# Hyena's output projection in the rings of the input projection, a finer last projection group, two pools for the convolution, and four early pairs of FFN products

## The chip, the cores and the metric

One core of a Trainium2 chip runs the whole kernel. The metric is the device time of one execution in microseconds (us). The engines are TensorE (PE: matmuls, with PEld for the weight load), VectorE (DVE), ScalarE (ACT), GpSimd (POOL) and SyncE (SP). SP and POOL issue the DMAs here, each from a queue that runs in order.

## The reference

One layer over 1024 latent tokens of width 1024, with a prefix of 256 context tokens, in float32:

```python
mod = silu(c) @ w_ada + b_ada                       # shifts, scales, gates
hc = modulate(rmsnorm(ctx), csh1, csc1)
k_c, v_c = split(hc @ w_in[:, 512:1536])
h = modulate(rmsnorm(x), sh1, sc1)
q, k, v, hv, hx1, hx2, gna, ghy = split(h @ w_in)   # w_in: 1024 x 5120
y_na = neighbourhood_attention(q, k, v, k_c, v_c, rpb)   # 8 heads of 64, windows 8 x 16 and all context keys
y_hy = hyena_mixer(hv, hx1, hx2, ...)               # order 2: z = gate[n] * long_conv_bidir(z, filter[n]), by FFT
x = x + g1 * ((sigmoid(gna) * (y_na @ w_na_o) + sigmoid(ghy) * (y_hy @ w_hy_o)) @ w_out)
h2 = modulate(rmsnorm(x), sh2, sc2)
x = x + g2 * ((silu(h2 @ w1) * (h2 @ w3)) @ w2)     # hidden 2816
return rmsnorm(x, final_g)
```

## The kernel before, in words

Each float32 operand is split into a high and a low part by one helper, `split` (L174 and L175): a cast on ScalarE, then a subtraction on VectorE. A product is then three matmuls for each 128 rows of depth (low by high, high by low, high by high), in `gemm` (L194) and in `product` (L1133).

The input projection (`project`) makes 40 blocks of 128 output channels. Each block has two halves of 512 tokens, `in_ps`, and each half is 24 matmuls of 128x512. ScalarE evacuates a half into `proj` (L601 and others), a tile of the ring "o" in the staging pool `self.stg`. The block's weights come by one 512 KB load (`wr`) in a ring of one, and are split into `wh` and `wl`. Transposed tokens (`tokens`) use the ring "tm" of the same pool.

The projection is a generator, and so are the filters, the modulation rows (`ada_rows`) and the long convolution (`conv`), which together are `side()`. The helper `_merged` advances the two in proportion: 39 projection steps to `SIDE` = 447 units of the side work. That, the scheduler's priorities and the pinned order of some matmuls set the order of instructions, in which the projection's halves lie between the small pieces of filters and convolution. When the convolution is through, `self.fine` is set, and the attention generator starts: it loads and rotates keys and queries (`kraw`, `qraw`, `kcraw` for context keys, all in a ring "raw" of two buffers), and the projection yields after the first half of a block and after the block. `AHEAD` = 5 projection steps go first, and then attention and projection take turns.

An attention step (there are 34, of which 32 have scores) issues the scores of its item (`s_ps`), the transpositions of the item before (`pt_ps`, L766), and the values of the item before that (L780). VectorE and ScalarE make the softmax between (L754, L755), and ScalarE copies `pts` (L770) and `yrow` (L787). What lies on TensorE between two such steps covers the softmax.

When the projection has ended, `hyena_out` loads the convolution's result `yhraw` in eight pieces (ring "g" of two buffers, shared with the gates `ghy`), splits it into `yhh` and `yhl`, and makes 16 products `hy_ps` of 12 matmuls. Their place is set by this rule of the attention's step number n:

```python
for n, _ in enumerate(attention):
    if n > 2 and n % 4 != 3 or n in (3, 19):
        next(hyena, None)
```

`mix` then makes `na_ps`, merges both branches by the gates and makes the output projection (`out_ps`). The FFN forms seven products of sums of the blocks of h2 and of weights in place of eight. `sums` makes those operands `h2_3` to `h2_7` on VectorE (in the profile and the order: `h_3h`, `h_3l` and so on). `ffn_early` does products that need only `h2_1` and `h2_2`, for three pairs of weight tiles w1 and w3, while the sums are made: four products of 12 matmuls (`x_ps`) a pair. Split weights lie in rings `oh` and `ol` of five. `ffn_up` follows with all the rest.

Of the kernel before, what the change touches and what calls it, by code (L numbers as in the profile page):

```python
# [10 lines left out]
F32 = mybir.dt.float32  # L11
# [12 lines left out]
SIDE = 447  # L24
# [134 lines left out]
class Block:  # L159
# [17 lines left out]
    def weights(self, pool, src, n=D, tag="w"):  # L177
        nc = self.nc
        raw = pool.tile([P, n], F32, tag=tag + "r", name=tag + "r")
        nc.sync.dma_start(raw, src)  # L180
        hi = pool.tile([P, n], F32R, tag=tag + "h", name=tag + "h")
        lo = pool.tile([P, n], F32R, tag=tag + "l", name=tag + "l")
        self.split(hi, lo, raw)
        return hi, lo
# [74 lines left out]
    def hidden(self, pool, wpool, mp, hid, w3, hT, hcT, psf):  # L259
# [42 lines left out]
        self.modulated(pool, psf, xs[0:4], 4, self.mod1[:, 0], hT[0][:, :, 0:512], hT[1][:, :, 0:512])  # L302
        normed(4, 4, "rstd1b")
        yield
        self.modulated(pool, psf, xs[4:8], 4, self.mod1[:, 0], hT[0][:, :, 512:T], hT[1][:, :, 512:T])
# [256 lines left out]
    def project(self, groups, wpool, psg, psc, hT, hcT, between):  # L562
# [8 lines left out]
        def half(f, w, st, ps, h):  # L571
# [4 lines left out]
            self.gemm(pt, w, hT, 8, 512, h * 512, self.pinned)  # L576
# [50 lines left out]
        for group in groups:  # L627
            ws = [self.ready.pop(f) for f in group]
            i = chunks.index(group[-1]) + 1
            if i < len(chunks) and chunks[i] not in self.ready:  # L630
                with self.tc.high_priority():
                    self.ready[chunks[i]] = self.weights(wpool, self.a["w_in"][chunks[i]])
# [9 lines left out]
            for f, w, st in zip(group, ws, sts):  # L642
                self.left -= 1
                finish(f, w, st)
                yield
# [3 lines left out]
    def attention(self, pool, kpool, prep, psums):  # L649
# [42 lines left out]
        def keys(pr):  # L692
            tl = tiles[pr]
            tl["kr"] = [prep.tile([P, T], F32R, tag=n, name=n, bufs=2) for n in ("krh", "krl")]
            x = prep.tile([P, 512], F32, tag="raw", name="kcraw", bufs=2)
            nc.sync.dma_start(x[:, 0:TC], self.kcd[pr])
            tl["kc"] = [prep.tile([P, TC], F32R, tag=n, name=n, bufs=2) for n in ("kch", "kcl")]
            self.split(*tl["kc"], x[:, 0:TC])
# [124 lines left out]
    def hyena_out(self, pool, wo, ps1):  # L823

        nc, a = self.nc, self.a
        yh = [pool.tile([P, 4, T], F32R, name=n, bufs=1) for n in ("yhh", "yhl")]
        for c in range(4):
            for h in range(2):
                sl = slice(h * 512, (h + 1) * 512)
                raw = pool.tile([P, 512], F32, tag="g", name="yhraw")  # L830
                nc.sync.dma_start(raw, self.yhd[c][:, sl])
                self.split(yh[0][:, c, sl], yh[1][:, c, sl], raw)
        yield
        for f in range(8):
            w = self.weights(wo, a["why"][f], 512, "wf")
            for h in range(2):
                sl = slice(h * 512, (h + 1) * 512)
                ps = ps1.tile([P, 512], F32, tag="f", name="hy_ps")
# [3 lines left out]
                nc.vector.tensor_tensor(g, ps, g, op=ALU.mult)  # L842
                nc.gpsimd.dma_start(self.hyd[f][:, sl], g)
# [4 lines left out]
    def ada_rows(self, pool, psf):  # L848
# [3 lines left out]
        for pair in ((3, 4), (2, 5)):  # L852
# [7 lines left out]
            for n, part in enumerate(pair):  # L860
                for k in range(8):
# [6 lines left out]
                    yield 0.8  # L868
# [17 lines left out]
    def run(self):  # L886
        tc, nc, a = self.tc, self.nc, self.a
        with ExitStack() as top:
# [19 lines left out]

            with ExitStack() as s1:
                E1 = s1.enter_context  # L910
                hpool = E1(tc.tile_pool(name="hT", bufs=1))
                hT = [hpool.tile([P, 8, T], F32R, name=n) for n in ("hTh", "hTl")]
                wpool = _Bufs(E1(tc.tile_pool(name="w", bufs=2)), wr=1)
# [10 lines left out]
                self.stg = E1(tc.tile_pool(name="stg", bufs=2))  # L924
                order = [[4, 5]] + [[f] for f in list(range(6, 24)) + list(range(4)) + list(range(32, 40)) + list(range(24, 32))]
                self.stc = first.enter_context(tc.tile_pool(name="stc", bufs=2, side="right"))
                with tc.tile_pool(name="mlp", bufs=1, side="right") as mp:
                    with tc.tile_pool(name="x0", bufs=1, side="right") as xp:
                        hidden = self.hidden(xp, wpool, mp, hid, w3, hT, hcT, psf)
                        next(hidden)  # L930
                        proj = self.project(order, wpool, psg, psc, hT, hcT, hidden)
                        next(proj)

                def side():
                    with tc.tile_pool(name="filt", bufs=3, side="right") as fp:
                        fgen = self.filters(_Bufs(fp, t4=1, mat=2, a=2, b=4), psf, hid, w3)
                        yield from _merged((fgen, 97), (self.ada_rows(fp, psf), 26))
# [21 lines left out]
                while self.left:  # L959
                    next(attention)  # L960
                    next(proj)

            with ExitStack() as s3:
                E3 = s3.enter_context
                rows = ExitStack()
                wf = _Bufs(rows.enter_context(tc.tile_pool(name="wf", bufs=2)), wfr=1)
                yp = rows.enter_context(tc.tile_pool(name="ya", bufs=1))
                g1 = yp.tile([P, D], F32, name="g1")
                nc.gpsimd.dma_start(g1, self.modd[2].broadcast_to((P, D)))
                self.ya = [yp.tile([P, 4, T], F32R, name=n) for n in ("yah", "yal")]  # L970
                with ExitStack() as s4:
                    E4 = s4.enter_context
                    ps1 = E4(tc.tile_pool(name="ps1", bufs=1, space=PSUM))
                    hp = E4(tc.tile_pool(name="hyo", bufs=2))
                    hyena = self.hyena_out(hp, wf, ps1)
                    next(hyena)
# [3 lines left out]
                    for _ in hyena:  # L980
                        pass
                    att.close()
# [446 lines left out]
```

## Time and profile before

| what | value |
|---|---|
| median of 3 runs | 1741.94 us (1740.68 to 1744.88) |
| the profiled execution: its own time | 1743.6 us |
| its span, first to last instruction | 1741.8 us |
| mean granted TensorE clock | 0.986 |
| busy: TensorE, VectorE, ScalarE, GpSimd | 1671.0, 1186.5, 661.3, 157.7 us |
| TensorE busy in 340 to 650 us (convolution and projection) | 309.98 us |
| VectorE busy in the same 310 us | 253.44 us |

The table is read stage by stage: TensorE's idle time is small in the sum, and the stretch where it lies matters. Around 690 us the attention starts, around 812 us the projection has ended, at 945 us the mix starts, and around 1110 us the early FFN products end.

### The profile page before, as it was taken

The numbers are of one execution on the slowest core, as the hardware profiler recorded it, in microseconds if no ns is written. First come the engines' busy times: TensorE is split into PE (matmuls) and PEld (weight loads), VectorE is DVE, ScalarE is ACT, GpSimd is POOL, SyncE is SP. The second block draws the span as 40 slices with busy tenths as digits, with TensorE's granted clock in tenths as the row PEclk, the third lists the DMA queues.
The fourth block names the chain that finished last, engine by engine and source line by source line (L and its number), as shares of the span: only waits on it lengthen the run. The fifth ranks groups of instructions, "written<-read, shape, count | busy, mean of one in ns | idle before, by whom it ended". The sixth has DMA issues, their size and how long they took to land.

```text
span 1741.8 us, 22929 instructions
## 1 busy us (share of the span) xinstructions
PE 1671.0 (96%) x8348; PEld 1316.8 (76%) x8348; DVE 1186.5 (68%) x2004; ACT 661.3 (38%) x1143; POOL 157.7 (9%) x281
## 2 busy tenths in 40 slices
PE   5999999999999999998999999899999999999997
PEld 2766766778777777787777888688888888877886
DVE  4566266699795956655965867867755656479567
ACT  4611222313122212545664225633343333344555
POOL 0100211101000004002200000000100000100000
PEclk8999999999999999998999999999999999999999
DMA  8375556645463437435757524333422322395344
GB/s 343 113 251 190 172 185 219 228 138 182 135 216 137 178 106 213 140 113 161 217 153 241 173 67 169 109 119 123 139 91 103 105 96 98 109 374 181 97 121 151
DMA packets 110758, 281.20 MB, mean 161 GB/s; under 512 B 15535, under 2 KB 24371, under 8 KB 108341
## 3 DMA queue, kind: packets, MB, share of 16 engines
q1 hardware_dynamic: 90584, 218.68, 37.6%
q0 software_dynamic: 19408, 60.61, 10.2%
q8 instruction: 66, 1.08, 0.3%
q10 hardware_dynamic: 653, 0.44, 0.1%
q14 instruction: 47, 0.39, 0.1%
HBM read 212.28 MB, written 67.39 MB: 161 GB/s over the span
## 4 chain that ended last, share of the span: by engine, by line
PE 46%; issue 23%; DMA 5%; DVE 4%; POOL 3%; ACT 2%; POOLq 0%; SPq 0%; DVEq 0%; ACTq 0%
PE in_ps L194 17%; PE dx_ps L1297 5%; PE out_ps L1071 4%; PE dft_ps L430 4%; PE dz_ps L1297 3%; PE x_ps L1133 2%; PE dft_ps L431 2%; PE dft_ps L432 2%; DMA w<-in_w 1%; PE na_ps L194 1%; POOL g L1245 1%; PE dy_ps L1297 1%; PE pt_ps L766 1%; POOL g L1239 1%; PE pt_ps L780 1%
## 5 line engine op out<-in xcount | busy, mean ns | idle before, releaser
L194 PE MATMUL in_ps<-hTh,wl 128*128 128x512 f32 x640 | 258.4, 404 | 5.7 <-ACT proj L601 5.7
L194 PE MATMUL in_ps<-hTl,wh 128*128 128x512 f32 x640 | 253.4, 396 | 0.0
L194 PE MATMUL in_ps<-hTh,wh 128*128 128x512 f32 x640 | 252.5, 395 | 0.0
L194 PEld LDWEIGHTS in_ps<-hTh,wl 128*128 128x128 f32 x640 | 121.6, 190 | 37.4 <-ACT proj L601 6.3
L194 PEld LDWEIGHTS in_ps<-hTh,wh 128*128 128x128 f32 x640 | 121.6, 190 | 26.7 <-issue 1.2
L194 PEld LDWEIGHTS in_ps<-hTl,wh 128*128 128x128 f32 x640 | 121.6, 190 | 25.6 <-issue 1.2
L175 DVE TENSOR_TENSOR wl<-wr,wh 128x1024 fp32r<-128x1024 f32 x40 | 48.9, 1222 | 78.2 <-ACT wh L174 78.1
L175 DVE TENSOR_TENSOR ol<-ws,oh 128x512 fp32r<-128x512 f32 x88 | 60.5, 688 | 55.4 <-ACT oh L174 55.2
L174 ACT CAST wh<-wr 128x1024 fp32r<-128x1024 f32 x40 | 41.9, 1048 | 138.2 <-PE in_ps L194 114.2
L175 DVE TENSOR_TENSOR ol<-ar,oh 128x512 fp32r<-128x512 f32 x77 | 52.8, 687 | 48.6 <-ACT oh L174 48.6
L174 ACT CAST oh<-ar 128x512 fp32r<-128x512 f32 x77 | 47.9, 622 | 85.1 <-PE dx_ps L1297 33.5
L174 ACT CAST oh<-ws 128x512 fp32r<-128x512 f32 x88 | 54.7, 622 | 53.4 <-PE x_ps L1133 23.2
L1297 PE MATMUL dx_ps<-ol,oh 128*128 128x512 f32 x176 | 68.8, 391 | 1.7 <-DVE ol L175 1.7
L1297 PE MATMUL dx_ps<-oh,ol 128*128 128x512 f32 x176 | 67.1, 391 | 3.2 <-DVE ol L175 3.2
L754 DVE CUSTOM_DVE_ANT_0 pe<-s_ps,bias 128x640 f32<-128x640 f32 x64 | 50.1, 819 | 29.3 <-PE s_ps L749 29.3
L1297 PE MATMUL dx_ps<-oh 128*128 128x512 f32 x176 | 68.5, 389 | 0.0
L430 PE MATMUL dft_ps<-a,matf 128*128 128x512 f32 x128 | 66.1, 598 | 1.5 <-DMA matf<-in_dft_f 1.5
L175 DVE TENSOR_TENSOR ol<-wr,oh 128x512 fp32r<-128x512 f32 x70 | 47.9, 688 | 28.6 <-ACT oh L174 28.5
L755 ACT ACTIVATE pe<-pe,mx 128x640 f32<-128x640 f32 x64 | 52.6, 822 | 37.3 <-DVE mx L754 37.1
L174 ACT CAST oh<-wr 128x512 fp32r<-128x512 f32 x70 | 43.1, 621 | 54.4 <-PE y_ps L1133 18.2
L358 DVE TENSOR_TENSOR fv<-filt_ps,dec 128x512 f32<-128x512 f32 x32 | 21.5, 689 | 50.9 <-DMA dec<-in_decay 31.4
L1073 DVE TENSOR_TENSOR x<-x,out_ps 128x512 f32<-128x512 f32 x64 | 42.8, 684 | 17.9 <-PE out_ps L1071 17.7
(392 smaller groups left out, 4219.7 us busy)
## 6 DMA issues: line engine op xcount, KB each, us to landing
wr<-in_w SPq DMA_DIRECT2D x50, 512.0 KB, 3.4
wr<-in_w_in SPq DMA_DIRECT2D x40, 512.0 KB, 4.5
ar<-g SPq DMA_DIRECT2D x77, 256.0 KB, 3.0
wal<-in_w_ada SPq DMA_DIRECT2D x32, 512.0 KB, 4.7
g<-t POOLq DMA_DIRECT2D x49, 256.0 KB, 3.0
matf<-in_dft_f SPq DMA_DIRECT2D x32, 384.0 KB, 5.4
bias<-in_rpb SPq DMA_DIRECT2D x64, 192.0 KB, 3.1
w<-in_w SPq DMA_DIRECT2D x44, 256.0 KB, 5.4
```

Of the source, the lines that this page charges most:

```text
L174: self.nc.scalar.copy(hi, src)
L175: self.nc.vector.tensor_sub(lo, src, hi.bitcast(F32))
L194: mm = nc.tensor.matmul(ps, ww[:, k * P:(k + 1) * P], xx[:, k, pos:pos + width], start=(i == 0), stop=(i == n - 1))
L430: nc.tensor.matmul(ps, m[:, 0], v.rearrange("p a b -> p (a b)"), start=True, stop=False)
L431: nc.tensor.matmul(ps[:, 0:256], m[:, 1], v[:, 1], start=False, stop=False)
L432: nc.tensor.matmul(ps[:, 256:512], m[:, 2], v[:, 0], start=False, stop=True)
L754: nc.vector.tensor_tensor_reduce(pe, ps[:, 256:896], bt, -1.0, 3e38, ALU.add, ALU.min, mx[:, 0:1])
L755: nc.scalar.activation(pe, pe, AF.Exp, bias=mx[:, 0:1], scale=-1.0, accum_out=mx[:, 1:2])
L1071: nc.tensor.matmul(ps, gg[x][:, tk], ww[y][:, sl], start=(i == 0), stop=(i == n - 1))
L1073: nc.vector.tensor_add(x1[:, sl], x1[:, sl], ps)
L1133: mm = nc.tensor.matmul(ps, w[u][:, k * P:(k + 1) * P], x[v][:, k, :], start=(start and k == 0 and i == 0), stop=(stop and k == 3 and i == 2),
L1297: nc.tensor.matmul(ps[j], x[u][:, j * P:(j + 1) * P], w[v], start=(start and i == 0 and c == 0), stop=(stop and i == N - 1 and k == len(re ...
```

## The change

- `hyena_out` takes its buffers from the projection's rings: the split rows stand in the pool of the first 512 tokens' operand (free after the last first half), the raw rows and `kcraw` in ring "tm", the gates in ring "o" as whole 512 KB tiles (one load and one store a block where there were two of 256 KB), the weights in the projection's weight ring, the products in the projection's bank.
- The operand `hT` is two tiles of 512 tokens in two pools. The last two blocks are one group, in the order first halves, then second halves, and the row loads start after its first halves.
- In fine mode the projection yields after every half, and each attention step after the projection's end takes one hyena product.
- `SIDE` is 496 and the modulation rows yield 1.2 units: the side work takes a smaller number of projection halves along.
- The convolution's buffers `v8` have a pool of their own.
- `ffn_early` makes four pairs; loads and splits of their weights have high priority, the ring p has eight buffers, and `junk2` stands in ring "t".

```diff
-SIDE = 447
+SIDE = 496
...
         for group in groups:
+            i = chunks.index(group[-1]) + 1
+            for f in (*group, *chunks[i:i + 1]):
+                if f not in self.ready:
+                    with self.tc.high_priority():
+                        self.ready[f] = self.weights(wpool, self.a["w_in"][f])
             ws = [self.ready.pop(f) for f in group]
...
             for h in range(2):
                 for f, w, st, ps in zip(group, ws, sts, pss):
                     half(f, w, st, ps, h)
-                if self.fine and not h:
-                    yield
+                    if self.fine:
+                        if h:
+                            self.left -= 1
+                            finish(f, w, st)
+                        yield
...
+                if group is groups[-1] and not h:
+                    then()
...
-            x = prep.tile([P, 512], F32, tag="raw", name="kcraw", bufs=2)
-            nc.sync.dma_start(x[:, 0:TC], self.kcd[pr])
+            x = self.stg.tile([P, 4, P], F32, tag="tm", name="kcraw")[:, 0:2].rearrange("p a b -> p (a b)")
+            nc.sync.dma_start(x, self.kcd[pr])
...
-        yh = [pool.tile([P, 4, T], F32R, name=n, bufs=1) for n in ("yhh", "yhl")]
+        yh = [pool.tile([P, 8, 512], F32R, tag=n, name=m).rearrange("p (c h) t -> p c (h t)", h=2)
+              for n, m in (("hTh", "yhh"), ("hTl", "yhl"))]
...
-                raw = pool.tile([P, 512], F32, tag="g", name="yhraw")
+                raw = self.stg.tile([P, 4, P], F32, tag="tm", name="yhraw").rearrange("p a b -> p (a b)")
...
         for f in range(8):
-            w = self.weights(wo, a["why"][f], 512, "wf")
+            g = self.stg.tile([P, T], F32, tag="o", name="ghy")
+            nc.sync.dma_start(g, self.gd[8 + f])
...
-                g = pool.tile([P, 512], F32, tag="g", name="ghy")
-                nc.sync.dma_start(g, self.gd[8 + f][:, sl])
-                nc.vector.tensor_tensor(g, ps, g, op=ALU.mult)
-                nc.gpsimd.dma_start(self.hyd[f][:, sl], g)
+                nc.vector.tensor_tensor(g[:, sl], ps, g[:, sl], op=ALU.mult)
+                if h:
+                    nc.gpsimd.dma_start(self.hyd[f], g)
+                    if f < 7:
+                        w = self.weights(wpool, a["why"][f + 1], 512)
...
-                    yield 0.8
+                    yield 1.2
...
-                    with tc.tile_pool(name="conv", bufs=4, side="right") as cp:
-                        cp = _Bufs(cp, t4=2, bp=2)
+                    with tc.tile_pool(name="conv", bufs=4, side="right") as cp, \
+                            tc.tile_pool(name="conv8", bufs=4, side="right") as c8:
+                        cp = _Bufs(cp, {"v8": c8}, t4=2, bp=2)
...
+                for _ in attention:
+                    next(hyena, None)
+                for _ in hyena:
+                    pass
...
-                    for n, _ in enumerate(attention):
-                        if n > 2 and n % 4 != 3 or n in (3, 19):
-                            next(hyena, None)
...
-                        wa = _Bufs(E3(tc.tile_pool(name="wA", bufs=1)), wr=2, oh=5, ol=5, p=6, t=9)
+                        wa = _Bufs(E3(tc.tile_pool(name="wA", bufs=1)), wr=2, oh=5, ol=5, p=8, t=9)
...
-                    early = self.ffn_early(wa, psf, h2, 3)
+                    early = self.ffn_early(wa, psf, h2, 4)
...
-                raw = self.raw_weight(wa, a[n][i])
-                ws.append([self.operand(wa, raw[:, sl]) for sl in (slice(0, 512), slice(512, D))])
+                with self.tc.high_priority():
+                    raw = self.raw_weight(wa, a[n][i])
+                    ws.append([self.operand(wa, raw[:, sl]) for sl in (slice(0, 512), slice(512, D))])
```

How instructions move is shown at three places; the names are tiles (out<-in), and a "x" at the end counts equal instructions in a row.

TensorE, behind the last projection half, before:

```order
L766 MATMUL pt_ps<-ident,pe 128x128 x10
L780 MATMUL pt_ps<-pts,vc 64x128 x4
L780 MATMUL pt_ps<-pts,v 64x128 x6
L746 MATMUL s_ps<-krh,qrl 128x384 x2
L746 MATMUL s_ps<-krl,qrh 128x384 x2
L746 MATMUL s_ps<-krh,qrh 128x384 x2
L749 MATMUL s_ps<-kch,ql 128x256 x2
L749 MATMUL s_ps<-kcl,qh 128x256 x2
L749 MATMUL s_ps<-kch,qh 128x256 x2
L766 MATMUL pt_ps<-ident,pe 128x128 x10
```

And now:

```order
L757 MATMUL s_ps<-kch,ql 128x256 x2
L757 MATMUL s_ps<-kcl,qh 128x256 x2
L757 MATMUL s_ps<-kch,qh 128x256 x2
L774 MATMUL pt_ps<-ident,pe 128x128 x10
L788 MATMUL pt_ps<-pts,vc 64x128 x4
L788 MATMUL pt_ps<-pts,v 64x128 x6
L194 MATMUL hy_ps<-yhh,wl 128x512
L194 MATMUL hy_ps<-yhl,wh 128x512
L194 MATMUL hy_ps<-yhh,wh 128x512
```

Before, three steps follow each other with no product between the scores and the next transpositions; now a hyena product stands behind the first step after the last half, and four projection halves more stand between the earlier steps.

ScalarE, at the start of the attention, before:

```order
L601 ACTIVATE proj<-in_ps 128x512
L174 CAST qh<-qraw 128x512
L601 ACTIVATE proj<-in_ps 128x512
L174 CAST qrh<-qraw 128x512
L174 CAST kch<-kcraw 128x256
L174 CAST wh<-wr 128x1024
L601 ACTIVATE proj<-in_ps 128x512
L174 CAST krh<-kraw 128x512
```

And now, at the end of the convolution:

```order
L473 COPY bp<-dft_ps 128x512
L602 ACTIVATE proj<-in_ps 128x512
L174 CAST kch<-kcraw 128x256 x2
L174 CAST wh<-wr 128x1024
L602 ACTIVATE proj<-in_ps 128x512
L544 COPY yhT<-yh_ps 128x512 x4
L174 CAST krh<-kraw 128x512
L602 ACTIVATE proj<-in_ps 128x512
```

The second pair's cast of the context keys has moved from among the queries to the first pair's, ahead of the transposed rows of the convolution (`yhT`).

VectorE, at the end of the sums, before:

```order
L175 TENSOR_TENSOR h_3l<-htmp,h_3h 128x512
L175 TENSOR_TENSOR h_6l<-h2raw,h_6h 128x512
L1119 TENSOR_TENSOR h2raw<-h2raw 128x512
L1164 TENSOR_TENSOR t<-x_ps,t 128x512
L175 TENSOR_TENSOR ol<-wr,oh 128x512
L175 TENSOR_TENSOR h_4l<-h2raw,h_4h 128x512
L175 TENSOR_TENSOR ol<-wr,oh 128x512 x4
L1193 TENSOR_TENSOR ws<-wr 128x512 x2
L1193 TENSOR_TENSOR ws<-ws,wr 128x512
```

And now:

```order
L175 TENSOR_TENSOR ol<-wr,oh 128x512
L1124 TENSOR_TENSOR h2raw<-htmp,h2raw 128x512
L175 TENSOR_TENSOR h_7l<-htmp,h_7h 128x512
L175 TENSOR_TENSOR h_3l<-htmp,h_3h 128x512
L175 TENSOR_TENSOR h_6l<-h2raw,h_6h 128x512
L175 TENSOR_TENSOR ol<-wr,oh 128x512
L1127 TENSOR_TENSOR h2raw<-h2raw 128x512
L1173 TENSOR_TENSOR t<-x_ps,t 128x512 x2
L175 TENSOR_TENSOR h_4l<-h2raw,h_4h 128x512
L175 TENSOR_TENSOR ol<-wr,oh 128x512 x2
L1202 TENSOR_TENSOR ws<-wr 128x512 x2
```

The weights' splits (`ol<-wr`), before four in a row behind the last sums, now stand among the sums, and the products' last step (`t<-x_ps,t`) of two pairs stands together at the end.

More of the change, by code (lines that the diff above doesn't have):

```diff
@@ L575, in half @@
             ps.append(pt)
[L576 removed]
+            self.gemm(pt, w, hT[h], 8, 512, 0, self.pinned)
             if f < 4:
@@ L907, in run @@
             self.setup(cpool)
+            rows = top.enter_context(ExitStack())
             with ExitStack() as s1:
[L910 to L913, printed above, removed]
+                E0, E1 = rows.enter_context, s1.enter_context
+                h1 = E0(tc.tile_pool(name="hT1", bufs=1))
+                wpool = _Bufs(E0(tc.tile_pool(name="w", bufs=2)), wr=1)
+                self.stg = E0(tc.tile_pool(name="stg", bufs=2))
+                h0 = E1(tc.tile_pool(name="hT0", bufs=1))
+                new = lambda p, m: [p.tile([P, 8, 512], F32R, tag=n, name=m + n[-1]) for n in ("hTh", "hTl")]
+                hT = [new(p, "hT") for p in (h0, h1)]
                 psg = [E1(tc.tile_pool(name="psg", bufs=1, space=PSUM))]
@@ L930, in run @@
                         next(hidden)
-                        proj = self.project(order, wpool, psg, psc, hT, hcT, hidden)
+                        hyena = self.hyena_out(h0, wpool, psg[0])
+                        proj = self.project(order, wpool, psg, psc, hT, hcT, hidden, lambda: next(hyena))
                         next(proj)
```

73 lines of the change are left out of this document (30 added, 43 removed).

## The prediction

> **What bounds the kernel now.** I read the page first.
>
> ```profile
> span 1741.8 us, 22929 instructions
> PE 1671.0 (96%) x8348; PEld 1316.8 (76%) x8348; DVE 1186.5 (68%) x2004; ACT 661.3 (38%) x1143; POOL 157.7 (9%) x281
> PEclk8999999999999999998999999999999999999999
> PE 46%; issue 23%; DMA 5%; DVE 4%; POOL 3%; ACT 2%; POOLq 0%; SPq 0%; DVEq 0%; ACTq 0%
> ```
>
> TensorE is busy 96% of the span and leads the chain that ended last. The change removes no matmul, so it can win only the 1741.8 − 1671.0 = 70.8 us in which TensorE stands idle, and the time lost where its clock is halved. So I asked next what TensorE waits for (us in total, times, longest).
>
> ```profile
> PE pt_ps L766 <- ACT yrow L787: 9.0, 5, 6.0
> PE x_ps L1133 <- DVE ol L175: 6.1, 1, 6.1
> PE in_ps L194 <- ACT proj L601: 5.7, 2, 3.3
> PE na_ps L194 <- DVE ghy L842: 1.7, 1, 1.7
> PE filt_ps L351 <- DVE fv L358: 5.0, 2, 3.7
> ```
>
> The first four are the waits that the change touches; the fifth stands for the rest, at the start and in the filters. A long one leaves more behind than its idle time, which a table of stretches shows (start:end, length, then busy us of TensorE, its weight load, VectorE, ScalarE, GpSimd; granted clock, DMA share, GB/s).
>
> ```profile
> 698.80:705.60 6.80, 5.79 (x14) 4.59 (x15) 5.36 (x11) 3.54 (x5) 2.19 (x4) 0.52 0.58 188
> 814.80:825.00 10.20, 5.74 (x36) 5.08 (x38) 6.46 (x16) 6.93 (x13) 0.00 (x0) 0.51 0.80 264
> 1117.50:1122.00 4.50, 4.47 (x11) 3.53 (x12) 1.75 (x4) 1.14 (x2) 0.00 (x0) 0.50 0.97 373
> 1150.00:1200.00 50.00, 50.00 (x220) 41.08 (x219) 38.76 (x61) 16.40 (x28) 7.01 (x13) 1.00 0.39 137
> ```
>
> The last row is the undisturbed rate: 50/220 = 0.227 us for a 128x512 matmul. In the others the clock is about 0.5, so half of TensorE's busy time there is lost: 2.9, 2.9 and 2.2 us.
>
> **The change part by part.**
>
> *1. Start of the attention.* SP's queue, ScalarE, then TensorE:
>
> ```profile
> 690.55 0.33 SPq L180 DMA_DIRECT2D wr<-in_w_in  x1
> 691.15 0.32 SPq L696 DMA_DIRECT2D kcraw<-kc  x1
> 693.69 0.62 ACT L174 CAST qrh<-qraw 128x512 fp32r<-128x512 f32 x1 [3.04 <-DVE qraw L677]
> 697.91 0.40 ACT L174 CAST kch<-kcraw 128x256 fp32r<-128x256 f32 x1 [3.60 <-DMA kcraw<-kc]
> 698.22 1.04 ACT L174 CAST wh<-wr 128x1024 fp32r<-128x1024 f32 x1
> 699.16 0.59 ACT L601 ACTIVATE proj<-in_ps 128x512 f32<-128x512 f32 x1
> 689.70 0.50 PE L194 MATMUL in_ps<-hTh,wl 128*128 128x512 f32 x1 [2.42 <-ACT proj L601]
> 699.81 0.80 PE L194 MATMUL in_ps<-hTh,wl 128*128 128x512 f32 x1 [3.29 <-ACT proj L601]
> ```
>
> The evacuation of a projection half stands on ScalarE behind the cast of the second pair's context keys. Their load had to wait for a place in the ring "raw", was issued at 691.15 and, by the wait in front of the cast, had landed only at 697.9. In the new order both context casts stand ahead of the evacuations, several halves earlier, since their loads use the token ring. That takes away 3.29 + 2.9 = 6.2 us. The wait of 2.42 stays: the cast of the rotated queries still stands ahead of an evacuation. Bounds: 0, if the weight cast behind kch is as late (its load was issued only 0.6 us before), and 2.42 + 6.2 = 8.6 if both waits go. I take −6.2, since kch is what the row names.
>
> *2. From the projection to the hyena output.*
>
> ```profile
> 816.49 0.62 ACT L174 CAST yhh<-yhraw 128x512 fp32r<-128x512 f32 x1 [3.62 <-DMA yhraw<-yh]
> 817.01 0.82 ACT L755 ACTIVATE pe<-pe,mx 128x640 f32<-128x640 f32 x1
> 818.94 0.26 ACT L787 COPY yrow<-pt_ps 128x128 f32<-128x128 f32 x1
> 819.26 2.40 PE L766 MATMUL pt_ps<-ident,pe 128*128 128x128 f32 x10 [6.05 <-ACT yrow L787]
> 830.18 1.31 PE L766 MATMUL pt_ps<-ident,pe 128*128 128x128 f32 x10 [0.90 <-ACT yrow L787]
> ```
>
> ScalarE waits for a load of the convolution's rows with the softmax of a step queued behind it, and TensorE has three steps without a product to put in. At stake: 6.05 + 0.90 idle and 2.9 of clock, 9.8 us. Afterwards the eight loads and splits begin two projection halves sooner, and every step holds a projection half of 24 matmuls or a hyena product of 12, 5.4 or 2.7 us, to cover the same ScalarE wait. It does not vanish: three casts stand in a row in front of the evacuation of a half, over two buffers, and each load is 256 KB.
>
> ```profile
> L831 SPq DMA_DIRECT2D yhraw<-yh x8: 326/326/522, 808.6 to 829.1; - x8
> DMA to landing us min/median/max: 2.7/2.9/7.5
> ```
>
> Before, the eight issues took 20.5 us. TensorE's own work of a step without a product is the distance of its scores to the next step's:
>
> ```profile
> 855.17 0.45 PE L746 MATMUL s_ps<-krh,qrl 64*128 64x384 f32 x2
> 858.74 0.69 PE L746 MATMUL s_ps<-krh,qrl 64*128 64x384 f32 x2
> ```
>
> 3.6 us, so that two steps with a half cover 2 × (5.4 + 3.6) = 18.0 us, and in the last loads' shadow another step without one follows. I leave 1.0 us of wait in front of the first hyena product, between 0 and the whole 9.8: −8.8. Behind ScalarE here queue the softmaxes and evacuations, and on SP's queue the bias loads behind the loads of rows.
>
> *3. Steps without a product.* Later in the hyena part the old pattern leaves three:
>
> ```profile
> PE pt_ps L766 <- ACT yrow L787: 2.1, 3, 1.1
> 861.29 1.39 PE L766 MATMUL pt_ps<-ident,pe 128*128 128x128 f32 x10 [1.14 <-ACT yrow L787]
> ```
>
> The first row is that wait in 845 to 935 us alone. With one product in each step 2.1 us go.
>
> *4. The tail.* The mix no longer starts on the bank that the last hyena product still held (1.7 us), but the last two attention steps now stand bare. One of them is of the kind in the row at 861.29: 1.1 us, and the mix's first loads may add some 0.4. Net −0.2, bounds −1.7 and +3.
>
> *5. Fourth early FFN pair.* VectorE, then TensorE:
>
> ```profile
> 1114.91 0.67 DVE L1164 TENSOR_TENSOR t<-x_ps,t 128x512 f32<-128x512 f32 x1
> 1115.51 0.67 DVE L175 TENSOR_TENSOR ol<-wr,oh 128x512 fp32r<-128x512 f32 x1
> 1116.11 0.67 DVE L175 TENSOR_TENSOR h_4l<-h2raw,h_4h 128x512 fp32r<-128x512 f32 x1
> 1116.71 1.27 DVE L175 TENSOR_TENSOR ol<-wr,oh 128x512 fp32r<-128x512 f32 x2
> 1117.53 0.76 PE L1133 MATMUL x_ps<-h_1h,ol 128*128 128x512 f32 x1 [6.15 <-DVE ol L175]
> ```
>
> TensorE has run through the third pair while VectorE, without a pause, is still at the sums; the splits of the next weights come behind them. A fourth pair gives four products of 12 matmuls, 4 × 12 × 0.227 = 10.9 us of TensorE, moved up from later work (its total stays), for four more splits of 0.60 us start to start, 2.4 us, that VectorE also had to make later. The splits now stand among the sums. Walking the new VectorE order with 0.60 us per operation, from the same start, the operands of the first product behind the four pairs come some 2 to 4 us before TensorE asks for them. So 6.15 + 2.2 = 8.4 go; bounds 0 (five buffers of oh and ol: ScalarE then stands behind TensorE for a buffer, with the sums queued behind it) and −8.4. I take −8.2.
>
> *6. The convolution pays.* Projection halves are TensorE's filler there; four of them, 4 × 24 × 0.227 = 21.8 us, go to the attention, where they displace idle time and not work.
>
> ```profile
> 340.00:450.00 110.00, 109.98 (x467) 82.99 (x466) 106.85 (x190) 26.15 (x37) 9.63 (x13) 1.00 0.54 177
> 450.00:560.00 110.00, 110.00 (x464) 84.92 (x463) 81.28 (x138) 24.18 (x34) 7.20 (x11) 1.00 0.45 153
> 560.00:680.00 120.00, 120.00 (x516) 93.50 (x515) 83.02 (x134) 26.68 (x41) 14.61 (x27) 1.00 0.48 159
> ```
>
> VectorE has 271 us of work in 340; 318 would still hold it. But in the first 110 us it has 3 us to spare, and this stretch loses its share, 110/340 × 21.8 = 7.1 us. If nothing slides into the next stretch, 7.1 − 3.1 = 4 us of TensorE idle follow. Bounds 0 and 21.8; I take +2, halfway to those 4, because the next 110 us have 29 us of VectorE room.
>
> *7. Edits that I cost at nothing:* the second pool for the convolution's buffers, which lets the rotary and key loads start without waiting for TensorE; one 512 KB gate load and store in place of two halves (off the path, a step ahead); the changed rates of filters and modulation rows, which end at the same projection step. The early wait of 3.7 us (filt_ps above) hangs on a load whose place among the others shifts: ±4, centre 0.
>
> *Sum:* −6.2 − 8.8 − 2.1 − 0.2 − 8.2 + 2 = −23.5. The profiled execution took 1743.6 us with a span of 1741.8; that gives 1720.1. It lies 1.7 above the median of 1741.94, from which I get 1718.4 and say 1718.5.
>
> The Trainium skill, "TensorE: Matmul & The Clock Gate", Part 1, states that the clock falls to half after at least one idle window of about 3.4 us, in free-running windows. The trace halves it after 3.29 us of idle and not after 2.42, which is a little stricter than that rule. By the rule's letter the wait of 3.29 would not have cost the 2.9 us of clock, and the sum would be −20.6; the granted clock of 0.52 decides for −23.5.
>
> **The rivals.**
>
> *A, slower: the convolution becomes VectorE's.* If its chain of transform, product and inverse keeps its length, all of the 21.8 us comes back as idle TensorE, and three of the new waits halve the clock at 2.9 us each, as above: +30.5 in place of +2, in all +5: 1747. It decides from 25.5 us of loss between 340 and 680 us on, which is the sum of the other parts. For it: 106.85 of 110, and the new order bunches eight transforms. Against it: the last two stretches have 66 us of room. By the page named above, waits shorter than a window would leave the clock alone, and A would give 1738.
>
> *B, partly: one or two of the waits only move.* Either the row loads still hold ScalarE longer than a half covers (part 2), or the FFN rings hold the splits back (part 5). Losing one gain of 8 to 9 gives 1727, two 1735.
>
> *C, no change:* all three big waits reappear one step later (loads that land after up to 7.5 us are as late against the new order): of the sum −2.1 − 0.2 + 2 are left, 1742, and 1738 to 1745 with part of one.
>
> **How the numbers follow.** Forecast 0.62, B 0.20, C 0.08, A 0.10. The forecast's own range is 1710 to 1725: with all good ends (−2.4 in part 1, −1.0 in 2, −1.5 in 4, −0.2 in 5, −2 in 6, −4 early) the time would be 11.1 less, 1707, of which I take in most. The range to hold 8 in 10 takes in B: 1709 to 1738. A change under 0.3% (5 us) is about what these runs cannot tell from none. Faster by more: 0.82; within: 0.08; slower: 0.10.
>
> **What would show it.** Right: the row x_ps <- ol gone or under 1 us; pt_ps <- yrow under 3 us in all; no clock below 0.9 between 690 and 1150 us; span minus busy near 50. Part 6: an idle total of TensorE between 340 and 660 us under 4. Wrong: a wait of dft_ps or yh_ps for VectorE in the list, x_ps <- ol still over 4 us behind the fourth pair, or hy_ps waiting for the casts of yhh.

## The result and the profile after

The changed kernel takes 1731.5 us (median of 7 runs, 1727.48 to 1734.75) beside 1744.06 us of the kernel before on the same chip: ratio 0.9921, 95% interval 0.9904 to 0.9938. By the ratio that is 13.8 us faster; the two medians lie 12.6 us apart. A second series on another chip gave 0.9908 (0.989 to 0.9926). The forecast was 23.5 us. The sign and the broad range of 1709 to 1738 held; the time lies outside the forecast's own range of 1710 to 1725, where the prediction had put rival B.

The page of the changed kernel's profiled execution (1732.6 us):

```profile
span 1730.8 us, 22902 instructions
PE 1670.6 (97%) x8348; PEld 1313.1 (76%) x8348; DVE 1189.5 (69%) x2008; ACT 659.7 (38%) x1139; POOL 153.0 (9%) x273
PEclk8999999999999999999999999999999999999999
PE 37%; issue 33%; DMA 4%; DVE 4%; POOL 3%; ACT 1%; SPq 0%; POOLq 0%; ACTq 0%; DVEq 0%
```

TensorE's idle time went from 70.8 to 60.2 us. The rows of TensorE's waits that bear on this (us in total, times, longest):

```profile
PE ar_ps L877 <- DMA wal<-in_w_ada: 8.4, 6, 3.1
...
PE filt_ps L351 <- DVE fv L358: 3.3, 3, 2.5
PE yh_ps L543 <- ACT yhT L544: 2.7, 1, 2.7
...
PE out_ps L1079 <- DVE ml L175: 1.8, 2, 1.5
PE pt_ps L788 <- ACT yrow L795: 1.5, 1, 1.5
PE hT_ps L1110 <- DVE x L1092: 1.4, 3, 0.9
PE ctx_ps L194 <- ACT projc L622: 1.4, 1, 1.4
PE hy_ps L194 <- ACT proj L602: 1.3, 1, 1.3
PE pt_ps L774 <- ACT yrow L795: 1.1, 1, 1.1
...
PE in_ps L194 <- ACT proj L602: 0.5, 1, 0.5
```

All four waits at which the change aimed are gone or small: x_ps <- ol (6.1 before) and na_ps <- ghy (1.7) have no row, pt_ps <- yrow fell from 9.0 to 1.1 and in_ps <- proj from 5.7 to 0.5. In their place stand six of 1 to 3 us that are new or have grown (yh_ps, out_ps, pt_ps of L788, hT_ps, ctx_ps, hy_ps), and beside the filters one grew by 3.7 us: ar_ps, the modulation rows, waiting for their weights. The largest of the six is at the end of the convolution (GpSimd, ScalarE, TensorE):

```profile
642.82 0.53 POOL L619 DMA_DIRECT2D gate<-proj  x1 [13.88 <-ACT proj L602]
645.31 0.59 ACT L544 COPY yhT<-yh_ps 128x512 f32<-128x512 f32 x1 [2.31 <-PE yh_ps L543]
649.63 0.58 ACT L544 COPY yhT<-yh_ps 128x512 f32<-128x512 f32 x1 [3.73 <-DMA gate<-proj]
650.27 0.66 PE L543 MATMUL yh_ps<-ident,yo 128*128 128x128 f32 x4 [2.69 <-ACT yhT L544]
```

The copy yhT needs a place in ring "o", which a gate store issued at 642.82 still holds; that store took 6.7 us to land, where the median of the seven between 600 and 700 us is 3.8. At the norm, the priority of the early pairs' weights had its price (VectorE, TensorE):

```profile
1086.22 0.69 DVE L175 TENSOR_TENSOR ol<-wr,oh 128x512 fp32r<-128x512 f32 x1
1086.82 0.75 DVE L1092 TENSOR_SCALAR x<-x,rstd 128x1024 f32<-128x1024 f32 x1
1087.62 1.05 PE L1110 MATMUL hT_ps<-ident,x 128*128 128x128 f32 x5 [0.94 <-DVE x L1092]
```

A weight split stands in front of the last of the norm's four scales, and the transpositions wait for that. Behind both places the clock was halved (same columns as the prediction's table of stretches):

```profile
650.80:654.20 3.40, 3.40 (x11) 2.68 (x10) 2.07 (x4) 1.60 (x3) 2.93 (x6) 0.54 0.48 172
1084.30:1087.70 3.40, 1.98 (x9) 1.09 (x9) 3.27 (x5) 0.62 (x1) 0.00 (x0) 1.00 0.38 145
1087.70:1091.10 3.40, 3.40 (x12) 2.82 (x13) 2.19 (x4) 3.08 (x5) 0.00 (x0) 0.54 0.48 154
```

To see where the time is, I cut TensorE's work into stages at the first or last instruction of a product, and subtracted what the stage's matmuls take at the distance that is the median of their kind in the kernel before. What is left is TensorE's loss: idle time, half clock, and matmuls that follow each other more slowly than that, together, in us of the profiled execution:

| stage | before | changed | changed, again | pool alone | hyena alone | FFN alone | best |
|---|---|---|---|---|---|---|---|
| start to last filt_ps | 57.2 | 60.6 | 59.4 | 55.5 | 62.4 | 60.0 | 55.2 |
| to last yh_ps (convolution) | 6.3 | 10.5 | 9.1 | 7.0 | 8.3 | 6.2 | 8.4 |
| to first na_ps (attention, hyena) | 40.0 | 25.9 | 23.9 | 29.8 | 34.7 | 41.3 | 25.6 |
| to first x_ps (mix) | 2.4 | 4.3 | 7.6 | 3.5 | 4.7 | 3.2 | 4.8 |
| to first z_ps (early FFN) | 10.1 | 3.8 | 3.8 | 10.2 | 9.6 | 2.2 | 1.1 |
| rest | 9.9 | 9.5 | 10.0 | 11.9 | 9.7 | 9.3 | 9.7 |
| sum | 125.9 | 114.6 | 113.8 | 117.9 | 129.4 | 122.2 | 104.8 |

The kernels of the other columns are those of the experiments below ("best" is the run combined2).

### The profile page after: what moved, and what is told of

It is laid out like the page before. It is cut to its first block, busy times and chain, and to the rows that moved or that the text cites. A ratio compares the mean times of both kernels' runs of the same rounds, so it can differ in the third digit from the quotient of the medians.

```text
span 1730.8 us, 22902 instructions
## 1 busy us (share of the span) xinstructions
PE 1670.6 (97%) x8348; PEld 1313.1 (76%) x8348; DVE 1189.5 (69%) x2008; ACT 659.7 (38%) x1139; POOL 153.0 (9%) x273
## 4 chain that ended last, share of the span: by engine, by line
PE 37%; issue 33%; DMA 4%; DVE 4%; POOL 3%; ACT 1%; SPq 0%; POOLq 0%; ACTq 0%; DVEq 0%
PE in_ps L194 8%; PE out_ps L1079 5%; PE dx_ps L1306 5%; PE x_ps L1141 4%; PE dz_ps L1306 3%; PE hy_ps L194 2%; PE pt_ps L788 2%; PE pt_ps L774 2%; DMA ar<-g 1%; POOL g L1254 1%; PE dft_ps L430 1%; PE dy_ps L1306 1%; PE s_ps L754 1%; POOL g L1248 1%; PE na_ps L194 1%
## 5 line engine op out<-in xcount | busy, mean ns | idle before, releaser
L175 DVE TENSOR_TENSOR wl<-wr,wh 128x1024 fp32r<-128x1024 f32 (+1 forms) x56 | 59.9, 1069 | 97.2 <-ACT wh L174 97.1
L174 ACT CAST wh<-wr 128x1024 fp32r<-128x1024 f32 (+1 forms) x56 | 51.8, 926 | 141.7 <-PE in_ps L194 108.7
```

The lines of the kernel that those rows point to most:

```text
L174: self.nc.scalar.copy(hi, src)
L175: self.nc.vector.tensor_sub(lo, src, hi.bitcast(F32))
```

## The experiments

Each ratio is to the kernel before on the same chip, with its 95% interval.

**FFN part alone on the kernel before.**

```diff
-                    early = self.ffn_early(wa, psf, h2, 3)
+                    early = self.ffn_early(wa, psf, h2, 4)
...
+                with self.tc.high_priority():
```

> The kernel before, with the FFN part of the change alone (four early pairs, their weights at high priority, eight buffers of p, the junk of the second norm in ring t). Theory of the trace after: the 6.15 us wait and its 2.2 us of clock go, but a weight split set between the norm's scales (TensorE waits 0.94 us there in the changed kernel) brings 0.7 us of wait and 1.7 us of half clock: 6 us faster than before, ratio 0.9965. Rival, the step of the prediction as it stood: 8.2 us faster, ratio 0.9953, no half clock near 1090 us. If the FFN part gives nothing, the ratio is 1.000 and the wait of x_ps for ol stands elsewhere.

Measured: 0.9936 (0.9915 to 0.9957), 1737.91 us. The wait for ol is gone, and nothing else of the old waits:

```profile
PE pt_ps L766 <- ACT yrow L787: 8.6, 5, 5.5
...
PE in_ps L194 <- ACT proj L601: 3.4, 2, 2.9
```

The FFN stage's loss fell from 10.1 to 2.2 us: 7.9 us, the prediction's 8.2 nearly. The ratio stands for 11.2 us (7.5 to 14.9), more than the stage accounts for; the prediction's 8.2 lies in that interval, the 6 of the theory does not. The norm's 0.94 us wait is there too, but this time no half clock followed it, so the theory's 6 us had counted a half clock that this execution did not have.

**Without the priority.**

```diff
-                with self.tc.high_priority():
-                    raw = self.raw_weight(wa, a[n][i])
+                raw = self.raw_weight(wa, a[n][i])
```

> The changed kernel without the high priority of the early pairs' weights, still four pairs. Theory: the pair alone does not help, since its own splits fall behind the sums again: TensorE waits about 6 us for ol ahead of the fourth pair, with half clock behind it, and the wait in the norm's transpositions (0.94 us and 1.7 us of clock) goes: some 5 us slower than the changed kernel, 1736 to 1738. Rival: the 10.9 us of the fourth pair cover the sums by themselves, and without the priority the norm is on time: 2.5 us faster than the changed kernel, 1729.

Measured: 0.9919 (0.9897 to 0.9941), 1734.29 us: in time not to be told from the changed kernel. The trace is clear, though:

```profile
PE x_ps L1141 <- DVE ol L175: 6.1, 1, 6.1
```

The whole wait is back, ahead of the fourth pair, and the stage's loss is 10.3 us. So without the priority the pair only moves the wait; the two belong together. The 5 us that were expected of the time did not come. That it does not show 6 us I put down to the earlier stages of that chip's runs (57.3 us of loss up to the filters in its profile, 60.6 in that of the changed kernel); this is argued, not shown.

**One pool.**

```diff
-                        cp = _Bufs(cp, {"v8": c8}, t4=2, bp=2)
+                        cp = _Bufs(cp, t4=2, bp=2)
```

> The changed kernel with the convolution's v8 buffers back in the one pool. Theory: the second pool lets the rotary, key and bias loads start while the last gate store is under way, and that store, 6.7 us long, holds the copy yhT on ScalarE, for which TensorE waits 2.7 us, with 1.7 us of half clock: with one pool that wait goes (-4.4 us), and the loads come some 10 us later, which brings back up to 6 us of waits for the evacuation at the start of the attention: 1727 to 1733, with the row yh_ps <- yhT gone or under 0.5 us. Rival: the wait comes from the halves taken out of the convolution, not from the pool: the row stays at 2 to 3 us, and the time is the same or later, 1731 to 1738.

Measured: 0.9942 (0.9921 to 0.9964), 1740.37 us. The time is, by the ratios, some 4 us longer than the changed kernel's, but the two intervals overlap. The row yh_ps <- yhT is gone, as the theory said, and the waits at the attention's start are there, larger than in the kernel before:

```profile
PE in_ps L194 <- ACT proj L602: 6.7, 2, 3.7
```

What differs ahead of them is seen in the loads of the rotary tables (SP's queue; count, durations in ns, first and last start), in the changed kernel and in this one:

```profile
L663 SPq DMA_DIRECT2D rope<-in_rope x2: 328/377/426, 636.9 to 637.3; - x2
```

```profile
L663 SPq DMA_DIRECT2D rope<-in_rope x2: 327/392/457, 653.6 to 654.0; - x2
```

The first scores start at 680.2 and 686.4 us, so the second pool brings these loads, and with them the rotation of keys and queries, from 33 to 43 us ahead of them. On the kernel before, the pool alone (the run after the next) brings them from 30.4 to 39.5 us ahead.

**The context keys back in ring raw.**

```diff
-            x = self.stg.tile([P, 4, P], F32, tag="tm", name="kcraw")[:, 0:2].rearrange("p a b -> p (a b)")
+            x = prep.tile([P, 512], F32, tag="raw", name="kcraw", bufs=2)[:, 0:TC]
```

> The changed kernel with the context keys' loads back in the ring raw of two. The prediction's step 1 (the second pair's kch, late by that ring, holds an evacuation): the wait of about 3.3 us with 2.9 us of half clock at the attention's start comes back, 5 to 6 us slower than the changed kernel. Rival, after the run with one pool, where the context keys used the token ring and waits of 3.1 and 3.7 us still came back: the second pool, with loads some 10 us earlier, is what took the waits away, and the ring matters by 1 us or less.

Measured: 0.9904 (0.9886 to 0.9922), 1729.22 us, beside 0.9908 of the changed kernel in the same series. The wait in_ps <- proj did not return:

```profile
PE yh_ps L543 <- ACT yhT L544: 2.5, 1, 2.5
...
PE in_ps L194 <- ACT proj L602: 0.5, 1, 0.5
```

The rival holds. All four combinations were run: without the second pool the wait is there with either ring (5.7 us with ring raw before, 6.7 with ring tm in the run with one pool), and with it the wait is gone with either (0.8 and 0.5 with ring raw, 0.5 with ring tm). The ring that step 1 of the prediction named had nothing to do with it.

**The second pool alone on the kernel before.**

```diff
-                    with tc.tile_pool(name="conv", bufs=4, side="right") as cp:
-                        cp = _Bufs(cp, t4=2, bp=2)
+                    with tc.tile_pool(name="conv", bufs=4, side="right") as cp, \
+                            tc.tile_pool(name="conv8", bufs=4, side="right") as c8:
+                        cp = _Bufs(cp, {"v8": c8}, t4=2, bp=2)
...
```

> The kernel before, with the second pool for the convolution's v8 buffers alone. Theory (the pool starts the attention's loads earlier): the waits in_ps <- proj at the attention's start, 5.7 us with 2.9 us of half clock, fall to under 1.5 us, and a wait yh_ps <- yhT of 1 to 3 us comes in: 4 to 7 us faster than before, ratio 0.996 to 0.9977. Rival, the prediction's step 1: without the token ring for the context keys the second wait of 3.3 us stays, and the ratio is 0.998 to 1.001.

Measured: 0.9973 (0.9958 to 0.9988), 1740.02 us. Waits of TensorE:

```profile
PE pt_ps L766 <- ACT yrow L787: 8.0, 6, 4.5
...
PE x_ps L1134 <- DVE ol L175: 6.1, 1, 6.1
...
PE yh_ps L543 <- ACT yhT L544: 0.9, 1, 0.9
PE in_ps L194 <- ACT proj L601: 0.8, 1, 0.8
```

One small edit of the change, costed at nothing, takes 10 us from the stage of attention and hyena (40.0 to 29.8). The stage shows about as much wherever the pool alone differs: 34.7 without it and 24.5 with it in the two hyena runs below. The whole time shows less here, 4.7 us by the ratio (2.1 to 7.3).

**The hyena part with the pool, and without it.** Both leave the FFN part out; the second has one pool as well.

```diff
-                        wa = _Bufs(E3(tc.tile_pool(name="wA", bufs=1)), wr=2, oh=5, ol=5, p=8, t=9)
+                        wa = _Bufs(E3(tc.tile_pool(name="wA", bufs=1)), wr=2, oh=5, ol=5, p=6, t=9)
...
-                    early = self.ffn_early(wa, psf, h2, 4)
+                    early = self.ffn_early(wa, psf, h2, 3)
...
-                with self.tc.high_priority():
...
```

> The changed kernel without its FFN part (three pairs, no high priority, six buffers of p): the second pool and the whole hyena part are left. By the traces, the second pool is worth 10 us between the convolution's end and the first na_ps, and the hyena part another 6: with 3 given back at the convolution's end and the mix, 11 to 13 us faster than before, ratio 0.9925 to 0.994. By the prediction's steps 1 to 4 and 6 (-15.3) it would be 0.991.

> The same with the convolution's buffers in one pool: the hyena part, the moved halves and the context keys in the token ring alone. Theory: without the pool the waits at the attention's start are there (6.7 us of idle and 5 us of half clock in the run with one pool, more than the 8.6 of before), and they eat what the hyena part gives: 0 to 4 us faster than before, ratio 0.998 to 1.000. Rival, steps 1 to 4 and 6 of the prediction, in which the pool does nothing: 15 us faster, 0.991.

Measured: 0.9949 (0.9933 to 0.9966), 1738.32 us with the pool, and 1.0005 (0.9988 to 1.0023), 1747.55 us without. On one chip, then, the pool alone makes 9.8 us of difference. With it, the gain falls a little short of the 11 to 13 us expected (the interval reaches them) and clearly short of the 15.3 of steps 1 to 4 and 6; without it, the theory's 0 to 4 us hold at their lower end. The part that names the change, together with the new rates, is worth nothing that can be measured without the pool. The rates take about 3 us from it (below), and no run has the part with the old rates and one pool. The trace of the run without the pool has the waits that it leaves:

```profile
PE in_ps L194 <- ACT proj L602: 7.1, 2, 4.1
...
PE x_ps L1141 <- DVE ol L175: 6.1, 1, 6.1
```

It does remove the 6 us at the transition (stage: 40.0 to 34.7) but loses some 5 up to the filters' end, 2 in the convolution and 2 in the mix. The FFN part (0.9936) and the rest with the pool (0.9949) would multiply to 0.9885, beside 0.9908 to 0.9921 of the whole; with intervals of 0.002 each way, these runs do not tell whether the parts get in each other's way.

**The rates of before.** Four projection halves go back into the convolution.

```diff
-SIDE = 496
+SIDE = 447
...
-                    yield 1.2
+                    yield 0.8
...
-                        yield from _merged((fgen, 97), (self.ada_rows(fp, psf), 39))
+                        yield from _merged((fgen, 97), (self.ada_rows(fp, psf), 26))
```

> The changed kernel with the rates of before (SIDE 447, modulation rows 0.8 and 26): four projection halves go back from the attention into the convolution, and four steps at the attention's end stand without a product. Theory: the moved halves are worth the bare steps that they fill, about 1.1 to 1.5 us each: 4 to 6 us slower than the changed kernel, 1736 to 1738; the wait yh_ps <- yhT stays, as the pool makes it. Rival (the convolution pays for the halves): the 4 us that the convolution's stretch lost come back, and the time is 1731 to 1733.

Measured: 0.9892 (0.9873 to 0.9912), 1730.85 us: not slower than the changed kernel but, if anything, faster. Both theories of it fail: the bare steps are there and cheap (4.4 us for six), and the convolution's stage does not gain (9.6 us of loss beside 9.1 to 10.5).

```profile
PE pt_ps L774 <- ACT yrow L795: 4.4, 6, 1.5
...
PE yh_ps L543 <- ACT yhT L544: 1.8, 1, 1.8
```

**The changed kernel again, and three that mend its new waits.** The first of the three takes the rates of before, gives the priority to the third and fourth pair only, and puts yhT into the second pool's ring.

```diff
-                with self.tc.high_priority():
+                with (self.tc.high_priority() if i > 1 else ExitStack()):
...
-            st = self.stg.tile([P, T], F32, tag="o", name="yhT")
+            st = pool.tile([P, 8, 256], F32, tag="v8", name="yhT").rearrange("p a b -> p (a b)")[:, :T]
```

> The changed kernel once more, on the same chip as the next three and as a second profile of it: 0.990 to 0.994 of the kernel before. The wait yh_ps <- yhT (2.7 us) and the 0.94 us in the norm's transpositions come again, since they hang on the order; the loss of clock behind them and the loss up to the filters' end (60.6 us over the plain matmul time, 57.2 before) differ from execution to execution by some 4 us.

> The changed kernel with the rates of before (SIDE 447, rows 0.8 and 26), high priority only for the third and fourth early pair, and yhT in the ring v8 of the second pool instead of ring o. If the two waits are what they were read to be, yh_ps <- yhT falls under 0.5 us and the 0.94 us in the norm's transpositions goes: 3 to 6 us faster than the changed kernel, 0.987 to 0.989 of the kernel before. Rival: the attention's loads now wait for the yhT stores in the pool that they follow, the evacuation waits at the attention's start come back, and it is 2 to 5 us slower than that.

> The run combined (rates of before, priority for the third and fourth pair only, yhT in the pool's ring v8) with the context keys back in ring raw. Theory: the keys of the last pair no longer queue behind the eight row loads in the token ring, 1 us of wait at the first hyena products goes: 0 to 2 us faster than combined, 0.987 to 0.989. Rival: no difference that five rounds can show.

> The same with the changed kernel's rates (SIDE 496, rows 1.2 and 39). The four moved halves fill the bare steps at the attention's end (some 4 us of idle in combined), but each half between two attention steps loses 0.5 us more than in the convolution: equal to combined2 within 2 us. The prediction's steps 3 and 6 as they stood would make the halves' move worth some 3 us.

Measured: the changed kernel 0.9908 (0.989 to 0.9926), 1730.52 us; combined 0.9889 (0.9871 to 0.9907), 1726.73 us; combined2 0.9868 (0.985 to 0.9886), 1722.87 us beside 1747.49 of the kernel before; combined496 0.9894 (0.9877 to 0.9912), 1727.28 us. The page of combined2:

```profile
span 1720.6 us, 22892 instructions
PE 1665.9 (97%) x8348; PEld 1308.7 (76%) x8348; DVE 1190.3 (69%) x2008; ACT 659.5 (38%) x1139; POOL 153.4 (9%) x273
```

The changed kernel's second profile has the 0.94 us in the norm's transpositions again, but the wait yh_ps <- yhT, expected at 2.7 us, was 1.0: so its size changes from execution to execution. In combined and combined2 that row is gone, and hT_ps <- x fell from 1.4 to 0.5 us; combined is 3.8 us faster than the changed kernel on the same chip (by the medians), as expected. combined2 beats both kernels, and reaches the time that the prediction had given the change, by edits that the prediction did not have. Whether its context keys add anything to combined is not shown: the wait that they were to remove has no row in combined either, and the two intervals overlap. combined2 and combined496 differ in the rates alone, by 4.4 us (no run of the one reaches those of the other), where at most 2 were expected; the difference lies up to the filters' end, as the last time in each row shows, the start of the last filt_ps, in combined2 and then in combined496:

```profile
L351 PE MATMUL filt_ps<-fw,hid x128: 376/376/480, 73.3 to 284.7; 64*128 64x256 f32 x128
```

```profile
L351 PE MATMUL filt_ps<-fw,hid x128: 376/376/792, 74.5 to 289.9; 64*128 64x256 f32 x128
```

Over all profiles the loss of that stage is 57.9 us in the mean of six kernels with the old rates (55.2 to 61.9) and 60.8 in that of eight with the new (57.3 to 65.7): a cost of some 3 us that these runs make likely, but single profiles overlap. Two rows of the waits do not overlap, and show where most of it lies. Before:

```profile
PE ar_ps L865 <- DMA wal<-in_w_ada: 4.7, 5, 2.2
...
PE ctx_ps L194 <- ACT projc L621: 0.3, 1, 0.3
```

In the six profiles with the old rates the modulation rows (ar_ps) wait 3.6 to 5.1 us for their weights, and in the eight with the new rates 5.7 to 8.6; ctx_ps waits 0.3 us in all of the first and 1.4 in all of the second.

## Why the prediction was right in its sign and short in its size

*Step 1 (−6.2).* The wait went, for another reason than the one given. The named ring changes nothing (0.9904 beside 0.9908); the second pool does it. The step read the cast at which ScalarE stood when TensorE ran dry, and not what had made the whole chain of loads and rotations late. The pool's worth in the stage is 10 us, more than the step's 6.2. That the chain was late because its loads were is read from their order in time; no run moved the loads by other means.

*Steps 2 to 4 (−8.8, −2.1, −0.2).* Mechanism right, size not: with the pool there, the hyena part takes the stage's loss from 29.8 to 24.5 us, 5 in place of 11. Two terms were mis-sized. First, less was at stake, since with the pool alone the wait at the transition is 4.5 us and not 6.05. Second, what stays is more than the 1.0 and 1.1 allowed for, as ScalarE and TensorE show in the changed kernel:

```profile
829.01 0.40 ACT L174 CAST kch<-kcraw 128x256 fp32r<-128x256 f32 x1 [1.39 <-DMA kcraw<-kc]
829.32 0.59 ACT L602 ACTIVATE proj<-in_ps 128x512 f32<-128x512 f32 x1
829.97 0.50 PE L194 MATMUL hy_ps<-yhh,wl 128*128 128x512 f32 x1 [1.25 <-ACT proj L602]
936.85 0.66 PE L788 MATMUL pt_ps<-pts,vc 128*64 128x128 f32 x8 [1.55 <-ACT yrow L795]
938.53 0.50 PE L194 MATMUL na_ps<-yah,wl 128*128 128x512 f32 x1 [0.36 <-ACT yrow L795]
```

The first hyena product shares its bank with the last projection half, whose evacuation stands behind the context keys, now in the queue of the eight row loads. With the wait of 1.14 us in the next step, 4.6 us stay idle between the last in_ps and the first na_ps. Moving the keys' loads back does not mend it: in that run other waits take the place of this one (hy_ps for ghy, 1.0 us), and 4.2 us stay idle, as in the changed kernel's second profile.

*Step 5 (−8.2).* Right: −7.9 in three kernels (the FFN part alone, one pool, the rates of before), −6.3 in the two profiles of the changed kernel and in the one with the keys moved back, in which 1.7 us of half clock followed the norm's wait. The order of VectorE that the prediction walked showed the split among the scales; the step did not look at what stands behind it.

*Step 6 (+2).* The convolution lost 3 to 4 us, not far from the +2, but not to VectorE, so that it is luck how near the size is: no wait of dft_ps for VectorE came in the changed kernel, and rival A had no ground. The wait for yhT, which comes with the second pool, is 2.7 of the 4.2 us in the first profile and 1.0 of the 2.8 in the second; with one pool that row is gone and the stage's loss is 8.0 us. Some 1.5 to 1.8 us over the 6.3 of before stay unexplained in all three. And the halves that were moved bring next to nothing in the stage of attention and hyena: against the rates of before its loss is 0.8 us more in one pair of profiles (the changed kernel and the run with the rates of before) and 0.9 less in the other (combined496 and combined2). Between the first scores and the last half the loss is 7.0 us with 12 halves and 9.4 with 16, 0.6 us for each half placed among scores and transpositions, nearly what a bare step waits.

*Step 7 (0).* This is the step that failed. The second pool was put at nothing and was the change's largest part: 10 us for it in the attention's stage, and 1 to 3 against it as the wait for yhT. The new rates cost about 3 us up to the filters' end, since the modulation rows wait longer for their weights; the prediction had allowed ±4 about 0. The mix lost 1.9 and 5.2 us in the two profiles, where step 4 allowed 0.4; why it differs so much stays open.

*Rivals and signs.* B gave the time (1727 to 1735), but by luck and not by its mechanism: none of the three big waits merely moved. What the change gave back came as the longer waits for the rows' weights and as six small waits elsewhere. Of the prediction's signs of being right, x_ps <- ol and pt_ps <- yrow came as named; the clock fell to 0.54 behind the norm's wait, and span minus busy is 60.2 and not near 50. By the sum of stages, −23.5 became −11.3 in the profile: attention and hyena −14.1 where −17.7 was due (steps 1 to 4 without the 0.4 of the mix), FFN −6.3, convolution +4.2, mix +1.9, filters +3.4, rest −0.4.

The Trainium skill's rule on the clock ("TensorE: Matmul & The Clock Gate", Part 1) says that its windows are free-running. The traces agree: within each trace, stretches of half clock begin whole multiples of 3.413 us apart, as at 651.06 and 1087.96 us in the changed kernel (128 of them) and at 699.02 and 815.08 in the kernel before (34). Idle time alone did not decide: a stretch just as busy, 1.98 us out of 3.40, was followed by half clock in the changed kernel and by full clock in the run with the old rates:

```profile
1083.00:1086.40 3.40, 1.98 (x11) 1.17 (x10) 2.88 (x5) 0.71 (x2) 0.00 (x0) 1.00 0.39 140
1086.40:1089.80 3.40, 3.40 (x20) 2.85 (x19) 2.58 (x5) 3.32 (x6) 0.00 (x0) 1.00 0.37 145
```

## What to carry to other kernels

Where a chain of loads, casts and rotations feeds the bottleneck, ask when its first load could start and what buffer it waits for; the instruction at which the engine stands when it runs dry may be the last link only. When a change takes away long waits on an engine that is 96% busy, sum the small waits that each edit can open (a ring place, a shared bank, a priority that overtakes), stage by stage: here six of 1 to 3 us, and one for loads that a changed rate had made longer, took half the gain. And test a bundle's parts alone: its headline part, with the rates that came with it, was worth nothing without a small edit to a buffer pool.

## What the runs showed of the hardware

A wait far shorter than 3 us can be followed by half clock: 0.94 us was the longest idle piece in the stretch from 1084.30 to 1087.70, in which TensorE was busy for 1.98 of 3.40 us, and the next 3.4 us ran at 0.54. The same wait in the norm left the clock alone in three of the six profiles that have it, so its price is a chance of 1.7 us and not a constant.

In these traces the halving goes with how busy TensorE is in a whole window of the 3.413 us grid. Cut on it, the fourteen traces hold some 5500 windows at full clock between 350 and 1715 us. All 20 with TensorE busy for 1.55 us or less were followed by half clock, none with more than 2.00 us was, and of the 45 between these two, 4 were. The prediction had read the trace by the length of a wait (3.29 us halves, 2.42 does not); in the kernel before, the window with most of the wait of 2.42 had 1.9 us of busy time, and the one with most of the wait of 3.29 had 0.9.
